# An RWKV-7 scan on one core: the transition and output matrices of each chunk made ahead of the states

## The chip, the cores and the metric

The kernel runs on one core of one Trainium2 chip. The metric is the device time of one execution in microseconds. TensorE (PE in the profile) multiplies, VectorE (DVE) and ScalarE (ACT) copy and do elementwise work, GpSimd (POOL) helps with splits, SyncE (SP) issues the DMAs. "Out<-in" in a row of the profile names the tile that is written and the tiles that are read.

## The reference

One layer of a hybrid encoder trunk on a sequence of 1024 with a width of 1024: an mLSTM branch, a Hyena branch and an RWKV-7 branch read the same normalised input, and their outputs are gated, projected and merged. The change is in the RWKV-7 branch, which scans in both directions over 16 heads of 64:

```python
def rwkv7_scan(r, w, k, v, kk, a, reverse):
    def step(state, inp):
        r_t, w_t, k_t, v_t, kk_t, a_t = inp
        sa = jnp.einsum('bhij,bhj->bhi', state, -kk_t)
        state = (state * w_t[:, :, None, :] + sa[..., None] * (kk_t * a_t)[:, :, None, :]
                 + v_t[..., None] * k_t[:, :, None, :])
        return state, jnp.einsum('bhij,bhj->bhi', state, r_t)
    ...
    y_fwd = rwkv7_scan(r_h, dec_h[:, :, 0], k_dir[:, :, 0], v_h, kk, a_h[:, :, 0], reverse=False)
    y_bwd = rwkv7_scan(r_h, dec_h[:, :, 1], k_dir[:, :, 1], v_h, kk, a_h[:, :, 1], reverse=True)
    y = head_norm(y_fwd + y_bwd, LNX_EPS) * heads(lnx_g) + heads(lnx_b)
```

## The kernel before

**Stages.** The trunk normalises and modulates the input, runs the mLSTM, then the Hyena branch, then the RWKV branch (`rwkv`, from about 830 to 1988 us of the profile), then the merge and the output projection. The input projection, 82 column tiles, is cut into jobs (`gemm`, the tile `pg`, lines 351 to 353: three products of 128x512 for each 128x128 piece of the weights, whose high and low parts ACT and POOL split in lines 333 and 334). Jobs fill TensorE beside the branches: `fill(n)` traces the next `n` pieces of the queue.

**The scan.** Heads are taken in eight pairs, two heads on the 128 partitions (h = 0 and 1). Both directions d of a pair run together. The 1024 positions are 16 chunks of 64; half a direction of a pair (g = 0 and 1) is eight chunks. For each pair `load` fetches k and r, `prep` (four calls: g and d) makes the decayed operands, `tphase` (once for each g) inverts the triangular 64x64 systems of 16 chunks and directions into `tt_t[g]`, `bonus` and `post` do what lies around the scan. `prep` writes `ar` (two halves: kk times decay, and r times decay) and `bk` (two halves: the delta rule's right side b over decay, and k over decay).

`setup(cx, b)` prepares a block b of two chunks, in two parts: the Gram products `pgr` of `bk` and `ar`, masked by DVE into `G`, with the first quarter of `G` overwritten by a copy of `ar` on ACT; then the transposes of `bk` through `ptv` into `B`, and, in the first four blocks, the values (`vp` times `cmat`) into `SV`, whose other half holds the state.

`scan` does 16 steps m, each for one chunk of either direction:

- `U` = products of `G` and `SV`; DVE copies it to `us` (line 1769);
- `SA` = products of `tt_t` and `us`; DVE and ACT copy it into the state's half of `SV` (lines 1775 and 1776);
- `SN` = products of `B` and `SV`; DVE adds the old state `S0` and multiplies by the chunk's decay `pc` (tile `sn`, through `tt`, line 476); DVE and ACT copy it into the next chunk's `SV` (lines 1800 and 1801);
- `own` and `states`, products of `SV` with `G` and of `S0` with `ar`, make the outputs `py`; they are issued one step late, behind `U` and `SA` of the next step. ACT copies them to `y`, or DVE adds them where the other direction was there first.

**Order.** `scan` is a generator with four yields a step. `weave` runs it and, at each yield, runs the generators that `rwkv` has put at that number (`put`: the rest of `prep` of this pair at 0 to 4, `tphase` of the second half at 6 to 26, `load`, `prep` and `tphase` of the next pair later) and an even share of the remaining jobs (`fill`). Between the yields of a step `next(ahead)` runs one part of the next block's `setup`. A scheduler then puts the instructions of each engine into one order at compile time; `in_turn` holds a group of products together (its first product stands in the trace under line 395, the others under 398), and `high_priority` and `issue_after` steer it. On the chip each engine takes its instructions in that order.

**PSUM.** `banks(name)` gives two banks of 512 from one buffer, the tag `a`, which `pq` and `pwx` of `tphase` and `pgr` and `ptv` of `setup` share one after the other. The steps' tile `pch` has two buffers of a bank, the jobs' `pg` three.

Of the kernel before, what the change touches and what calls it, by code (L numbers as in the profile page):

```python
# [18 lines left out]
T = 1024  # L19
# [266 lines left out]
class Trunk:  # L286
# [1060 lines left out]
    def rwkv(self, yc_out, pairs=range(8)):  # L1347
        nc, tc, A = self.nc, self.tc, self.A
        with ExitStack() as c2:
# [17 lines left out]
            self.gmask = cp.tile([128, 2, 128], F32, name="gmask")  # L1367
            nc.sync.dma_start(self.gmask, A["gmask"])
# [21 lines left out]
            cx = [dict(p=p, ar={}, al={}, bk={}, pc={}) for p in pairs]  # L1390
# [10 lines left out]
            for i in range(n):  # L1401
# [7 lines left out]
                put(ahead(tc, self.tphase(cx[i], 1), TP), *range(6, 28, 2))  # L1409
                if i + 1 < n:  # L1410
# [4 lines left out]
                    put(ahead(tc, self.tphase(nx, 0), TP), *range(39, 62, 2))  # L1415
# [118 lines left out]
    def prep(self, cx, g, d):  # L1534
# [46 lines left out]
        for q in range(2):  # L1581
            ar = self.ep.tile([128, 4, 2, CL], F32, name="ar", tag="ar", bufs=8)
            bk = self.ep.tile([128, 4, 2, CL], F32, name="bk", tag="bk", bufs=8)
            cs = slice(4 * q, 4 * q + 4)
            self.stt(ar[:, :, 0, :], c8(rd(kk))[:, cs], -2.0, P[:, cs, 0:64], MUL, MUL)
            self.tt(ar[:, :, 1, :], c8(rd(r))[:, cs], P[:, cs, 1:65])
            self.tt(bk[:, :, 0, :], c8(tmp)[:, cs], s[:, cs, 1:65])

            self.tt(bk[:, :, 1, :] if d == 0 else bk[:, :, 1, ::-1], c8(a)[:, cs], s[:, cs, 1:65])
            for j in range(2):  # L1590
                cx["al"][g, d, 2 * q + j] = ar[:, 2 * j:2 * j + 2, 0, :]
            for j in range(4):
                cx["ar"][g, d, 4 * q + j] = ar[:, j]
                cx["bk"][g, d, 4 * q + j] = bk[:, j]
            yield

    def tphase(self, cx, g):
# [68 lines left out]
    def setup(self, cx, b):  # L1666

        nc, rp, vp = self.nc, self.rp, self.vp
        if b == 0:
# [4 lines left out]
        ops = [(j, d, cx["bk"][g, d, c + j], cx["ar"][g, d, c + j]) for j in range(2) for d in range(2)]  # L1674

        G = rp.tile([128, 2, 2, 2, 128], F32, name="G", tag="G", bufs=2)

        pg = [x.rearrange("p (j d c) -> p j d c", j=2, d=2) for x in self.banks("pgr")]
        self.in_turn(partial(nc.tensor.matmul, pg[h][:, j, d, :], bk[hsl[h]], ar[hsl[h]], start=True, stop=True)
                     for j, d, bk, ar in ops for h in (1, 0))  # L1680
        for h in range(2):
            self.tt(G[:, :, :, h, :], pg[h], self.gmask.unsqueeze(1).broadcast_to([128, 2, 2, 128]))
            for d in range(2):
                nc.scalar.copy(G[0:64, :, d, h, 0:64], cx["al"][g, d, b % 4][hsl[h]])  # L1684
        yield

        B = rp.tile([128, 2, 2, 128], F32, name="B", tag="B", bufs=2)
        pt, pv = self.banks("ptv")  # L1690
        pt = pt.rearrange("p (j d c) -> p j d c", j=2, d=2)
        for j, d, bk, ar in ops:
            nc.tensor.transpose(pt[:, j, d, :], bk.rearrange("p a b -> p (a b)"), self.ident)
        nc.scalar.copy(B, pt)
        if b < 4:

            SV = rp.tile([128, 2, 4, 64], F32, name="SV", tag="SV", bufs=4)
            if b == 0:
                nc.gpsimd.memset(SV[0:64], 0.0)
# [5 lines left out]
            for k in range(2):  # L1705
                nc.scalar.copy(SV[64:128, :, 2 * k:2 * k + 2].rearrange("p h e x -> p e h x"),
# [6 lines left out]
        cx["set"] = (G, B, SV, at)  # L1713
        yield

    def outputs(self, y, py, m, S0, ar, now):

        nc = self.nc
        hsl = (slice(0, 64), slice(64, 128))
        G, B, SV, at, both = now  # L1720

        def own(ins):
            return self.in_turn((partial(nc.tensor.matmul, py[hsl[h], d], SV[:, h, at[d]], G[:, m % 2, d, h, 64:128],
                                         start=m == 0 or d == 0, stop=m == 0)
                                 for d in range(2) for h in range(2)), ins)

        def states(ins):
            self.in_turn((partial(nc.tensor.matmul, py[hsl[h], d], S0[hsl[h], d], ar[d][hsl[h], 1, :],
                                  start=False, stop=d == 1)
                          for d in range(2 if m else 0) for h in range(2)), ins)  # L1730
# [7 lines left out]
        return own, states  # L1738

    def scan(self, cx, nx):  # L1740

        nc, rp = self.nc, self.rp
        S0 = None
        y = rp.tile([128, T], F32, name="y", tag="y", bufs=1)
        hsl = (slice(0, 64), slice(64, 128))

        def chunk(m):

            G, B, SV, at = cx["set"]
            at = at[m % 2]  # L1750
            step = at[1] - at[0]
            return G, B, SV, at, slice(at[0], at[1] + (1 if step > 0 else -1) if at[1] + step >= 0 else None, step)
        now, late = chunk(0), None
        for m in range(16):
            g, c, j = m // 8, m % 8, m % 2
# [160 lines left out]
```

## Time and profile before

| | us |
|---|---|
| median of 3 runs | 2189.37 |
| lowest and highest | 2178.8, 2193.34 |
| the profiled execution | 2200.05 |
| its span from the first to the last instruction | 2198.3 |
| the scan, first step to last, in the profile | 929.5 to 1988 |

The profile records one execution. A row of a view by groups has line, engine, operation, tiles, shape and count, then busy time in us and the mean of one in ns, then the idle time of the engine ahead of it and what ended it. A row of the timeline begins with start and length in us. "128*64 128x64" of a product is its tile of the array, rows times columns, and the shape of what streams through it. One fp32 product of the program is two instructions. A waits row has the waiting engine and line, what it waited for, then us in total, times, and the longest.

### The profile page before, as it was taken

The numbers are of one execution on the slowest core, as the hardware profiler recorded it, in microseconds if no ns is written. First come the engines' busy times: TensorE is split into PE (matmuls) and PEld (weight loads), VectorE is DVE, ScalarE is ACT, GpSimd is POOL, SyncE is SP. The second block draws the span as 40 slices with busy tenths as digits, with TensorE's granted clock in tenths as the row PEclk, the third lists the DMA queues.
The fourth block names the chain that finished last, engine by engine and source line by source line (L and its number), as shares of the span: only waits on it lengthen the run. The fifth ranks groups of instructions, "written<-read, shape, count | busy, mean of one in ns | idle before, by whom it ended". The sixth has DMA issues, their size and how long they took to land. (4 is left out here: it accounts for less than half of the span.)

```text
span 2198.3 us, 45984 instructions
## 1 busy us (share of the span) xinstructions
PE 1994.0 (91%) x17098; PEld 1509.2 (69%) x17098; DVE 1634.6 (74%) x4754; ACT 1103.2 (50%) x2558; POOL 424.3 (19%) x485
## 2 busy tenths in 40 slices
PE   6999899999989899899989999999898887897998
PEld 4666777787868677666766676666666665675786
DVE  4854999988447947788787888868887888764536
ACT  5557356454242115664665756667466564532221
POOL 2211311122222432311101111111114411010200
PEclk9999999999999999999998999999899998897999
DMA  8211222334465345321322333224143542445623
GB/s 255 70 67 59 78 77 90 112 101 127 143 200 172 119 138 163 124 68 61 130 79 93 117 106 102 92 81 136 52 155 118 187 144 63 159 143 175 196 89 129
DMA packets 169384, 262.19 MB, mean 119 GB/s; under 512 B 17863, under 2 KB 87335, under 8 KB 169160
## 3 DMA queue, kind: packets, MB, share of 16 engines
q1 hardware_dynamic: 169160, 259.25, 36.3%
q8 instruction: 135, 2.21, 0.4%
q14 instruction: 89, 0.73, 0.1%
HBM read 181.06 MB, written 78.12 MB: 118 GB/s over the span
## 5 line engine op out<-in xcount | busy, mean ns | idle before, releaser
L334 POOL TENSOR_TENSOR wl<-wraw,wh 128x256 fp32r<-128x256 f32 x408 | 371.5, 915 | 1488.6 <-ACT wh L333 1464.8
L351 PE MATMUL pg<-hh,wh 128*128 128x512 f32 x1440 | 601.5, 418 | 20.9 <-ACT wh L333 11.8
L352 PE MATMUL pg<-hh,wl 128*128 128x512 f32 x1440 | 594.3, 413 | 16.4 <-POOL wl L334 16.3
L353 PE MATMUL pg<-hl,wh 128*128 128x512 f32 x1440 | 592.4, 412 | 1.9 <-DVE hl L565 1.8
L351 PEld LDWEIGHTS pg<-hh,wh 128*128 128x128 f32 x1440 | 278.7, 194 | 88.9 <-ACT wh L333 15.1
L352 PEld LDWEIGHTS pg<-hh,wl 128*128 128x128 f32 x1440 | 279.3, 194 | 78.0 <-POOL wl L334 22.2
L353 PEld LDWEIGHTS pg<-hl,wh 128*128 128x128 f32 x1440 | 278.1, 193 | 62.0 <-DVE hl L565 2.8
L333 ACT CAST wh<-wraw 128x256 fp32r<-128x256 f32 x408 | 162.7, 404 | 220.6 <-PE pg L353 122.1
L476 DVE TENSOR_TENSOR tm<-Ab,Tb 128x126 f32<-128x126 f32 (+22 forms) x496 | 145.4, 293 | 4.4 <-DMA Tb<-in_tinit 2.7
L476 DVE TENSOR_TENSOR Tb<-Tb,tm 128x126 f32<-128x126 f32 (+22 forms) x496 | 144.2, 291 | 1.9
L473 DVE SCALAR_TENSOR_TENSOR st<-pg,hmu,st 128x511 f32<-128x511 f32 (+1 forms) x130 | 80.9, 636 | 27.9 <-ACT e L424 17.6
L476 DVE TENSOR_TENSOR G<-pgr,gmask 128x512 f32<-128x512 f32 x128 | 85.4, 679 | 17.0 <-PE pgr L398 17.0
L457 ACT ACTIVATE st<-pg 128x512 f32<-128x512 f32 x74 | 44.2, 597 | 99.9 <-PE pg L353 95.0
L1684 ACT COPY G<-ar 64x128 f32<-64x128 f32 x256 | 64.3, 295 | 48.4 <-DVE G L476 46.6
L473 DVE SCALAR_TENSOR_TENSOR st<-st,pg 128x512 f32<-128x512 f32 x80 | 54.3, 679 | 35.7 <-PE pg L353 12.7
L398 PE MATMUL pgr<-ar,bk 64*128 64x128 f32 x896 | 76.9, 287 | 0.0
L141 DVE SCALAR_TENSOR_TENSOR row<-row 64x1 f32<-64x1 f32 x393 | 72.7, 208 | 2.1
L1769 DVE COPY us<-pch 128x128 f32<-128x128 f32 x128 | 36.3, 283 | 45.8 <-PE pch L398 45.5
L395 PEld LDWEIGHTS pch<-SV,G 128*64 128x64 f32 x256 | 25.3, 139 | 65.5 <-ACT SV L1801 52.3
L395 PE MATMUL pch<-SV,G 128*64 128x64 f32 x256 | 43.2, 252 | 27.7 <-ACT SV L1801 26.2
L476 DVE TENSOR_TENSOR dw<-dw,dw 128x512 f32<-128x512 f32 x92 | 67.1, 760 | 0.9
L395 PEld LDWEIGHTS pch<-SV,B 128*64 128x64 f32 x256 | 25.3, 139 | 60.1 <-ACT SV L1776 50.1
(677 smaller groups left out, 4228.4 us busy)
## 6 DMA issues: line engine op xcount, KB each, us to landing
wraw<-in_w_in SPq DMA_DIRECT2D x340, 128.0 KB, 2.3
low<-lora SPq DMA_DIRECT2D x32, 512.0 KB, 4.1
sig<-st SPq DMA_DIRECT2D x48, 256.0 KB, 2.6
st<-sig SPq DMA_DIRECT2D x48, 256.0 KB, 3.5
wraw<-in_w_br SPq DMA_DIRECT2D x68, 128.0 KB, 2.8
adw<-in_ada_w SPq DMA_DIRECT2D x16, 512.0 KB, 7.1
x<-in_x SPq DMA_DIRECT2D x8, 512.0 KB, 6.1
hx<-st SPq DMA_DIRECT2D x16, 256.0 KB, 2.0
```

The costliest lines, as they stand in the source:

```text
L141: self.ops.append(lambda: self.nc.vector.scalar_tensor_tensor(o, a, s, b, op0=op0, op1=op1))
L333: self.nc.scalar.copy(hi, raw)
L334: self.nc.gpsimd.tensor_tensor(lo, raw, hi.bitcast(F32), op=SUB)
L351: nc.tensor.matmul(p, wh, hh, start=(k == 0), stop=False)
L352: nc.tensor.matmul(p, wl, hh, start=False, stop=False)
L353: nc.tensor.matmul(p, wh, hl, start=False, stop=(k == n - 1))
L395: ins = f()
L398: ins = f()
L457: self.nc.scalar.activation(o, p, AF.Tanh, scale=0.5)
L473: return self.nc.vector.scalar_tensor_tensor(out, in0, s, in1, op0=op0, op1=op1)
L476: return self.nc.vector.tensor_tensor(out, a, b, op=op)
L1684: nc.scalar.copy(G[0:64, :, d, h, 0:64], cx["al"][g, d, b % 4][hsl[h]])
```

## The change

The state's half and the value's half of `SV` change places. For each chunk and direction the setup now makes the transition matrix `R` (128x64: from state and values to the next state before decay) and the output matrix `Q` (128x64: from state and values to the outputs), and a step has only the products `SN` = R and `SV`, and `py` = `SV` and Q. `SN` is scaled by `pc` while it is copied into the next chunk's `SV`: two scaled copies on ACT for the first head, one on DVE for the second. `U`, `SA`, `us`, the state tile `sn`, and the late outputs are gone.

`setup` has three parts instead of two, each in its own place between yields (the third in the block's second step). First: the products of `ar` with `ki` (tile `px`) and of `be` with `ar` and with the unit matrix (`pb`); DVE masks half of each into `X` and `Gb`, ACT copies the other half. Second: `tt` times `X` into `TX`, and the values. Third: products of `ki` with `ar` and with the unit matrix, and of `TX` with `Gb` added to them, in `pqr`; ACT copies `R`, DVE masks `Q`. So `tt` is read in the setup, not in the step, and `tphase` is put at earlier numbers. `bk` becomes `be` (b over decay) and `ki`, eight standing tiles whose second half POOL fills once with the unit matrix. `tphase` takes the diagonal exchange of its partitions (`o` for `64 * h`) with the same number of products.

```diff
             nc.vector.tensor_scalar(self.hwa, self.col("w0", 0, 32), 0.5, None, op0=MUL)
             self.hlgb = cp.tile([128, 16], F32, name="hlgb")
             nc.vector.tensor_scalar(self.hlgb, self.col("lg", 0, 16), 0.5, None, op0=MUL)
-            self.gmask = cp.tile([128, 2, 128], F32, name="gmask")
-            nc.sync.dma_start(self.gmask, A["gmask"])
+            gm = cp.tile([128, 8, CL], F32, name="gmask")
+            nc.sync.dma_start(gm, A["gmask"])
+            self.mask_x, self.mask_g, self.mask_q, self.eye = gm[:, 0:2], gm[:, 2], gm[:, 3:7], gm[:, 7]
+            self.ki = [self.ep.tile([128, 4, 2, CL], F32, name="ki", tag="bk", bufs=8) for _ in range(8)]
+            for x in self.ki:
+                nc.gpsimd.tensor_copy(x[:, :, 1, :], self.eye.unsqueeze(1).broadcast_to([128, 4, CL]))
...
-                put(ahead(tc, self.tphase(cx[i], 1), TP), *range(6, 28, 2))
+                put(ahead(tc, self.tphase(cx[i], 1), TP), 6, 8, 10, 12, 13, 14, 15, 16, 18, 20, 22)
...
-                    put(ahead(tc, self.tphase(nx, 0), TP), *range(39, 62, 2))
+                    put(ahead(tc, self.tphase(nx, 0), TP), 39, 40, 41, 42, 43, 44, 46, 48, 50, 52, 54)
...
             ar = self.ep.tile([128, 4, 2, CL], F32, name="ar", tag="ar", bufs=8)
-            bk = self.ep.tile([128, 4, 2, CL], F32, name="bk", tag="bk", bufs=8)
+            be = self.ep.tile([128, 4, CL], F32, name="be", tag="be", bufs=8)
+            ki = self.ki[4 * g + 2 * d + q]
             cs = slice(4 * q, 4 * q + 4)
             self.stt(ar[:, :, 0, :], c8(rd(kk))[:, cs], -2.0, P[:, cs, 0:64], MUL, MUL)
             self.tt(ar[:, :, 1, :], c8(rd(r))[:, cs], P[:, cs, 1:65])
...
+            self.tt(be, c8(tmp)[:, cs], s[:, cs, 1:65])
+            self.tt(ki[:, :, 0, :] if d == 0 else ki[:, :, 0, ::-1], c8(a)[:, cs], s[:, cs, 1:65])
             for j in range(4):
                 cx["ar"][g, d, 4 * q + j] = ar[:, j]
-                cx["bk"][g, d, 4 * q + j] = bk[:, j]
+                cx["be"][g, d, 4 * q + j] = be[:, j]
+                cx["ki"][g, d, 4 * q + j] = ki[:, j]
...
@@ -1665,69 +1672,122 @@
     def setup(self, cx, b):
         nc, rp, vp = self.nc, self.rp, self.vp
         if b == 0:
             nc.sync.dma_start(vp, self.krv["v", cx["p"]])
             cx["sv"] = []
         g, c = b // 4, 2 * (b % 4)
         hsl = (slice(0, 64), slice(64, 128))
...
+        ops = [(2 * j + d, 8 * d + c + j) + tuple(cx[n][g, d, c + j] for n in ("ar", "be", "ki"))
+               for j in range(2) for d in range(2)]
+        mm = lambda o, l, r, start=True, stop=True: partial(nc.tensor.matmul, o, l, r, start=start, stop=stop)
+        px, pb = (x.rearrange("p (i c) -> p i c", c=128) for x in self.banks("pxb"))
+        def grams():
+            for i, u, ar, be, ki in ops:
+                for h in range(2):
+                    yield mm(px[hsl[1 - h], i], ar[hsl[h], 0, :], ki[hsl[h]].rearrange("p a b -> p (a b)"))
+                for h in range(2):
+                    yield mm(pb[hsl[h], i, 0:64], be[hsl[h]], ar[hsl[h], 1, :])
+                for h in range(2):
+                    yield mm(pb[hsl[h], i, 64:128], be[hsl[h]], self.eye[hsl[h]])
+        self.in_turn(grams())
+        X = rp.tile([128, 4, 128], F32, name="X", tag="X", bufs=1)
+        Gb = rp.tile([128, 4, 128], F32, name="Gb", tag="Gb", bufs=1)
+        dm = lambda x: x.rearrange("p (j d) t -> p j d t", d=2)
+        self.tt(dm(X[:, :, 0:64]), dm(px[:, :, 0:64]), self.mask_x.unsqueeze(1).broadcast_to([128, 2, 2, CL]))
+        nc.scalar.copy(X[:, :, 64:128], px[:, :, 64:128])
+        self.tt(Gb[:, :, 0:64], pb[:, :, 0:64], self.mask_g.unsqueeze(1).broadcast_to([128, 4, CL]))
+        nc.scalar.copy(Gb[:, :, 64:128], pb[:, :, 64:128])
         yield
-        B = rp.tile([128, 2, 2, 128], F32, name="B", tag="B", bufs=2)
+        tt = self.tt_t[g]
         pt, pv = self.banks("ptv")
-        pt = pt.rearrange("p (j d c) -> p j d c", j=2, d=2)
-        for j, d, bk, ar in ops:
-            nc.tensor.transpose(pt[:, j, d, :], bk.rearrange("p a b -> p (a b)"), self.ident)
-        nc.scalar.copy(B, pt)
+        pt = pt.rearrange("p (i c) -> p i c", c=128)
+        self.in_turn(mm(pt[hsl[h], i], tt[hsl[1 - h], u, :], X[hsl[1 - h], i]) for i, u, *_ in ops for h in range(2))
+        TX = rp.tile([128, 4, 128], F32, name="TX", tag="X", bufs=1)
+        nc.scalar.copy(TX, pt)
         if b < 4:
             SV = rp.tile([128, 2, 4, 64], F32, name="SV", tag="SV", bufs=4)
             if b == 0:
-                nc.gpsimd.memset(SV[0:64], 0.0)
+                nc.gpsimd.memset(SV[64:128], 0.0)
             cx["sv"].append(SV)
             pv = pv[:, 0:256].rearrange("p (e c) -> p e c", e=2)
             for e in range(2):
                 t0 = 128 * (7 - b if e else b)
                 nc.tensor.matmul(pv[:, e], vp[:, t0:t0 + 128], self.cmat, start=True, stop=True)
             for k in range(2):
-                nc.scalar.copy(SV[64:128, :, 2 * k:2 * k + 2].rearrange("p h e x -> p e h x"),
+                nc.scalar.copy(SV[0:64, :, 2 * k:2 * k + 2].rearrange("p h e x -> p e h x"),
                                pv[hsl[k]].rearrange("p e (h x) -> p e h x", h=2))
             at = ((0, 3), (2, 1))
             SV = cx["sv"][b]
         else:
             SV = cx["sv"][7 - b]
             at = ((1, 2), (3, 0))
-        cx["set"] = (G, B, SV, at)
         yield
-    def outputs(self, y, py, m, S0, ar, now):
-        nc = self.nc
+        pq = [x.rearrange("p (i c) -> p i c", c=128) for x in self.banks("pqr")]
+        def both():
+            for i, u, ar, be, ki in ops:
+                for n, r in enumerate((ar[:, 1, :], self.eye)):
+                    for h in range(2):
+                        yield mm(pq[h][:, i, 64 * n:64 * n + 64], ki[hsl[h]].rearrange("p a b -> p (a b)"), r[hsl[h]],
+                                 i + n == 0, False)
+            for i, *_ in ops:
+                for h in range(2):
+                    yield mm(pq[h][:, i], TX[hsl[h], i], Gb[hsl[h], i], False, i == 3)
+        self.in_turn(both())
+        R = rp.tile([128, 2, 4, CL], F32, name="R", tag="R", bufs=2)
+        Q = rp.tile([128, 2, 4, CL], F32, name="Q", tag="Q", bufs=1)
+        for h in range(2):
+            nc.scalar.copy(R[:, h], pq[h][:, :, 64:128])
+            self.tt(Q[:, h], pq[h][:, :, 0:64], self.mask_q)
+        cx["set"] = (Q, R, SV, at)
+        yield
+    def scan(self, cx, nx):
+        nc, rp = self.nc, self.rp
+        y = rp.tile([128, T], F32, name="y", tag="y", bufs=1)
         hsl = (slice(0, 64), slice(64, 128))
...
+        def chunk(m):
+            Q, R, SV, at = cx["set"]
+            at = at[m % 2]
+            step = at[1] - at[0]
+            return Q, R, SV, at, slice(at[0], at[1] + (1 if step > 0 else -1) if at[1] + step >= 0 else None, step)
+        now = chunk(0)
+        for m in range(16):
+            g, c, j = m // 8, m % 8, m % 2
+            Q, R, SV, at, _ = now
+            if j == 0:
+                ahead = self.setup(cx, m // 2 + 1) if m < 14 else self.setup(nx, 0) if nx else iter(())
+            ch = self.ps.tile([128, 2, 2, CL], F32, name="pch", tag="c", bufs=2)
+            SN, py = ch[:, 0], ch[:, 1]
+            ins = None
+            if m < 15:
+                ins = self.in_turn(partial(nc.tensor.matmul, SN[hsl[h], d], R[:, h, 2 * j + d], SV[:, h, at[d]],
+                                           start=True, stop=True) for d in range(2) for h in range(2))
+            self.in_turn((partial(nc.tensor.matmul, py[hsl[h], d], SV[:, h, at[d]], Q[:, h, 2 * j + d],
+                                  start=True, stop=True) for d in range(2) for h in range(2)), ins)
+            yield
+            next(ahead, None)
+            yield
+            if m < 15:
+                now = chunk(m + 1)
+                SV, at, to = now[2:]
+                pc = cx["pc"][g][:, :, c:c + 1]
+                for d in range(2):
+                    nc.scalar.activation(SV[64:128, 0, at[d]], SN[0:64, d], AF.Copy, scale=pc[0:64, d])
+                self.tt(SV[64:128, 1, to], SN[64:128], pc[64:128].broadcast_to([64, 2, CL]))
             for d, n in enumerate((m, 15 - m)):
                 ysl = y[:, 64 * n:64 * n + 64]
                 src = py[:, d] if d == 0 else py[:, d, ::-1]
...
```

The steps that follow in `scan` (the outputs into `y` and the last two yields) stand as before. `gmask` on the host becomes the four masks and the unit matrix.

More of the change, by code (lines that the diff above doesn't have):

```diff
@@ L1389, in rwkv @@
             n = len(pairs)
-            cx = [dict(p=p, ar={}, al={}, bk={}, pc={}) for p in pairs]
+            cx = [dict(p=p, ar={}, be={}, ki={}, pc={}) for p in pairs]
             run(self.load(cx[0]))
@@ L1673, in setup @@
         hsl = (slice(0, 64), slice(64, 128))
[L1674 to L1684, printed above, removed]
+        ops = [(2 * j + d, 8 * d + c + j) + tuple(cx[n][g, d, c + j] for n in ("ar", "be", "ki"))
+               for j in range(2) for d in range(2)]
@@ L1737, in states @@
                     self.tt(ysl, ysl, src, ADD)
[L1738 to L1755, printed above, removed]
-            tt = self.tt_t[g]
-            ar = [cx["ar"][g, d, c] for d in range(2)]
-            G, B, SV, at, both = now
-            if j == 0:
-                ahead = self.setup(cx, m // 2 + 1) if m < 14 else self.setup(nx, 0) if nx else iter(())
-            ch = self.ps.tile([128, 4, 2, CL], F32, name="pch", tag="c", bufs=2)
-            U, SA, SN, py = (ch[:, i] for i in range(4))
-            ins = self.in_turn(partial(nc.tensor.matmul, U[hsl[h], d], G[:, j, d, h, 0:64], SV[:, h, at[d]],
-                                       start=True, stop=True) for d in range(2) for h in (1, 0))
-            if late:
-                late[0](ins)
-            us = self.sm.tile([128, 2, CL], F32, name="us", tag="us", bufs=2)
-            nc.vector.tensor_copy(us, U)
-            ins = self.in_turn(partial(nc.tensor.matmul, SA[hsl[h], d], tt[hsl[h], 8 * d + c, :], us[hsl[h], d],
-                                       start=True, stop=True) for d in range(2) for h in range(2))
-            if late:
-                late[1](ins)
-            late = None
-            nc.vector.tensor_copy(SV[0:64, 0, both], SA[0:64])
-            nc.scalar.copy(SV[0:64, 1, both], SA[64:128])
-            yield
-            next(ahead, None)
-            yield
-            self.in_turn(partial(nc.tensor.matmul, SN[hsl[h], d], B[:, j, d, hsl[h]], SV[:, h, at[d]],
-                                 start=True, stop=True) for d in range(2) for h in (1, 0))
-            S1 = self.sm.tile([128, 2, 64], F32, name="sn", tag="sn", bufs=3)
-            pc = cx["pc"][g][:, :, c:c + 1].broadcast_to([128, 2, 64])
-            if m == 0:
-                self.tt(S1, SN, pc)
-            else:
-                self.tt(S1, SN, S0, ADD)
-                self.tt(S1, S1, pc)
-            late = self.outputs(y, py, m, S0, ar, now)
-            S0 = S1
-            if m < 15:
-                now = chunk(m + 1)
-            if m in (7, 15):
-                late[1](late[0](None))
-                late = None
-            if m < 15:
-                SV, at = now[2], now[4]
-                nc.vector.tensor_copy(SV[0:64, 0, at], S1[0:64])
-                nc.scalar.copy(SV[0:64, 1, at], S1[64:128])
```

32 lines of the change are left out of this document (12 added, 20 removed).

## The prediction

> **What bounds the kernel now.** The page comes first:
>
> ```profile
> PE 1994.0 (91%) x17098; PEld 1509.2 (69%) x17098; DVE 1634.6 (74%) x4754; ACT 1103.2 (50%) x2558; POOL 424.3 (19%) x485
> ```
>
> TensorE looks full, but its products are pipelined and the record counts their tails, so this 91% bounds nothing. What the change touches runs from 929.5 to 1988 us, eight pairs of heads of 16 steps each; the groups by tile show that nothing on `pch`, `G` or `B` lies before or after it, save one setup. The busy times by window, cut where a pair's first `us` copy starts, with a stretch before the phase as the last row (columns: length, then busy time and count of PE, weight loads, DVE, ACT, POOL, granted clock, DMA):
>
> ```profile
> 929.50:1055.70 126.20, 117.88 (x1547) 86.88 (x1547) 99.73 (x312) 68.47 (x183) 17.54 (x24) 0.95 0.23 77
> 1055.70:1193.30 137.60, 125.55 (x1566) 93.35 (x1566) 108.49 (x324) 82.57 (x204) 17.08 (x23) 0.93 0.29 93
> 1193.30:1323.30 130.00, 122.15 (x1586) 89.51 (x1588) 105.56 (x319) 85.08 (x205) 16.43 (x23) 1.00 0.33 107
> 1323.30:1459.50 136.20, 127.50 (x1603) 93.29 (x1599) 109.75 (x329) 83.13 (x207) 22.11 (x28) 1.00 0.31 101
> 1459.50:1594.10 134.60, 120.50 (x1552) 89.18 (x1554) 111.16 (x325) 84.31 (x203) 14.98 (x22) 0.94 0.27 87
> 1594.10:1750.40 156.30, 135.25 (x1607) 98.64 (x1609) 131.47 (x326) 99.78 (x238) 56.41 (x61) 0.96 0.46 149
> 1750.40:1884.70 134.30, 115.11 (x1523) 85.23 (x1525) 111.45 (x332) 75.82 (x187) 15.09 (x21) 0.90 0.37 119
> 1884.70:1988.00 103.30, 93.71 (x1192) 68.39 (x1192) 67.56 (x203) 44.55 (x128) 10.02 (x13) 0.93 0.42 135
> ...
> 660.00:740.00 80.00, 75.32 (x319) 60.61 (x319) 65.65 (x89) 19.47 (x42) 24.33 (x25) 0.98 0.55 173
> ```
>
> DVE is busy for 0.79, 0.79, 0.81, 0.81, 0.83, 0.84 and 0.83 of the first seven pairs and 0.65 of the last. For TensorE I count what its instructions occupy, from start to start, in the timeline of one step:
>
> ```profile
> 1210.43 0.27 PE L395 MATMUL pch<-SV,G 128*64 128x64 f32 x1 [0.80 <-ACT SV L1801]
> ...
> 1211.05 0.51 PE L353 MATMUL pg<-hl,wh 128*128 128x512 f32 x1
> ...
> 1211.71 0.27 PE L395 MATMUL pch<-us,tt 64*64 64x64 f32 x1
> 1211.72 0.27 PE L398 MATMUL pch<-us,tt 64*64 64x64 f32 x1
> ...
> 1212.33 0.50 PE L352 MATMUL pg<-hh,wl 128*128 128x512 f32 x1
> ...
> 1214.78 0.27 PE L395 MATMUL pch<-SV,B 128*64 128x64 f32 x1 [1.04 <-ACT SV L1776]
> ...
> 1215.16 0.50 PE L1552 MATMUL plw<-low,w2h 128*128 128x512 f32 x1
> 1215.50 0.60 PE L1693 MATMUL ptv<-ident,bk 128*128 128x128 f32 x4
> 1215.85 0.48 PE L1552 MATMUL plw<-low,w2l 128*128 128x512 f32 x1
> ...
> 1216.40 0.39 PE L352 MATMUL pg<-hh,wl 128*128 128x512 f32 x1
> 1216.63 0.39 PE L353 MATMUL pg<-hl,wh 128*128 128x512 f32 x1
> ...
> 1218.35 0.71 PE L1704 MATMUL ptv<-cmat,vp 128*128 128x128 f32 x4
> 1218.81 0.48 PE L351 MATMUL pg<-hh,wh 128*128 128x512 f32 x1
> ...
> 1220.98 0.37 PE L395 MATMUL pgr<-ar,bk 64*128 64x128 f32 x1
> ...
> 1222.07 0.27 PE L395 MATMUL pch<-SV,B 128*64 128x64 f32 x1
> ```
>
> A wide product (128x512) occupies 0.23 us (1216.40 to 1216.63). The products `U` with the outputs `own` take 0.62 (1210.43 to 1211.05), `SA` with `states` 0.62 (1211.71 to 1212.33), `SN` 0.38 (1214.78 to 1215.16): 1.62 a step. A block of two steps adds its Gram products (`pgr`) 1.09, four transposes 0.35, and in half of the blocks the value products 0.46. `tphase` adds:
>
> ```profile
> 1467.47 0.24 PE L395 MATMUL pq<-ar,bk 64*32 64x64 f32 x1
> ...
> 1469.38 0.27 PE L395 MATMUL pch<-us,tt 64*64 64x64 f32 x1
> ```
>
> Its 128 products take 1.91 us; its two groups of 64 I put at 1.2 each by that row. A pair thus has 16 x 40 scan instructions, 8 x 20 of setup, 16 of values and 512 of `tphase`, about 1,320 in all, which occupy 16 x 1.62 + 8 x 1.44 + 4 x 0.46 + 2 x 4.3 = 48 us. The rest of the PE count in a window row are wide products: 227, 246, 266, 283, 232, 287 and 203. The pairs hold 100, 105, 109, 113, 101, 114 and 95 us of work for TensorE, together 737 of 955 us: 0.79, 0.76, 0.84, 0.83, 0.75, 0.73 and 0.70 of their length.
>
> So **two engines are near their limit together**. Pairs 5 to 7 have little for TensorE and are no shorter: there DVE, at 0.83 to 0.84, sets the time. In pairs 3 and 4 both stand above 0.8. What is left is waiting for one another:
>
> ```profile
> DVE us L1769 <- PE pch L398: 45.5, 45, 3.5
> PEld pch L395 <- ACT SV L1801: 52.3, 71, 5.8
> PEld pch L395 <- ACT SV L1776: 50.1, 82, 2.2
> ```
>
> The reader sees a round trip: PE waits for a copy, whose engine waits for PE, three times a step.
>
> **The change part by part.** *Steps.* `U`, `SA`, `SN`, `own` and `states` (40 instructions) become `SN` and the outputs (16 of the `SV,G` kind, 0.62). TensorE saves 1.0 us a step, 2.0 a block. Two of three round trips go.
>
> *Setup.* Gone are `pgr` and the transposes, 1.44. In come three groups.
>
> The first has 24 products in 64x64 tiles, 48 instructions. All four tiles are used, each for about 0.22 us per chunk and direction: two of the 0.11 that a pair takes in `pgr` (1.09 for eight pairs, less some 0.2 of start), or four half as wide. `pq` shows that tiles of one row group run beside each other: 128 products in 1.91 us is 15 ns each, which two at a time would not reach. So 4 x 0.23 + 0.2 of start = 1.15; two tiles at a time would give 2.0.
>
> The second (`TX`) has 16 instructions 128 wide, like `pgr`: 1.09.
>
> The third has 32 instructions 64 wide and 16 that are 128 wide, all with 128 columns of weights. What do 128 columns cost when little streams through them?
>
> ```profile
> L737 PEld LDWEIGHTS pdc<-de,ident x16: 183/187/189, 273.4 to 275.1; 64*128 64x128 f32 x16
> ```
>
> Sixteen products of only 8 columns start from 273.4 to 275.1 us, 0.113 apart, as slow as 128 columns do: the weight load sets the pace. So 24 pairs of two row groups at 0.111 + 0.2 = 2.85; if the load were hidden, 2.0. I take 2.85, for this row has the same 64x128 weights.
>
> A block's setup goes from 1.44 to 5.09 and its steps from 3.24 to 1.24: **+1.65 us of TensorE a block** (0.8 to 2.5), 13 us a pair.
>
> Here a page speaks against the change. The Trainium skill, TensorEngine Tiling (Array Packing), Restrictions and Gotchas, says that different row tiles cannot access one PSUM bank at the same time. By it the first two groups would run one row group at a time. The rows speak against that: `us,tt` has both row groups writing one bank, and its first two products start 10 ns apart (1211.71, 1211.72).
>
> *DVE.* Out go:
>
> ```profile
> L476 DVE TENSOR_TENSOR G<-pgr,gmask 128x512 f32<-128x512 f32 x126 | 84.1, 678 | 15.9 <-PE pgr L398 15.9
> L476 DVE TENSOR_TENSOR sn<-sn,pc 128x128 f32<-128x128 f32 x120 | 37.3, 311 | 0.6
> L1769 DVE COPY us<-pch 128x128 f32<-128x128 f32 x128 | 36.3, 283 | 45.8 <-PE pch L398 45.5
> L1775 DVE COPY SV<-pch 64x128 f32<-64x128 f32 x128 | 35.3, 276 | 25.5 <-PE pch L398 24.5
> L476 DVE TENSOR_TENSOR sn<-pch,sn 128x128 f32<-128x128 f32 x120 | 34.0, 283 | 39.1 <-PE pch L398 32.7 <-ACT st L457 5.0 <-ACT wh L333 0.8
> L1800 DVE COPY SV<-sn 64x128 f32<-64x128 f32 x120 | 27.3, 228 | 1.2 <-PE pch L398 0.7
> ```
>
> That is 254 us. In come four masked copies of 128x256 a block; between 0.283 for 128 elements and 0.678 for 512 this is 0.41 each, 106 us in all, and one scaled 64x128 copy a step, 0.28 x 120 = 34. Net -114, 14 a pair; the records of neighbours overlap a little, so -90 is the lower end. DVE falls from 845 to about 731 us.
>
> *ACT.* Out go:
>
> ```profile
> L1684 ACT COPY G<-ar 64x128 f32<-64x128 f32 x252 | 63.3, 295 | 48.1 <-DVE G L476 46.3
> L1694 ACT COPY B<-ptv 128x512 f32<-128x512 f32 x63 | 36.8, 584 | 19.5 <-PE ptv L1693 18.9
> ```
>
> 100 us, and two `SV` copies a step for two scaled ones of half the width, about even. In come four 128x256 copies (0.37 each by interpolation) and one 128x512 (0.58) a block, 132. ACT rises by some 30 from 624 of 1058, which DVE and PE cover; without that cover it is late by those 30.
>
> *Queues.* `tphase` must end some steps earlier, since setup now reads `tt`; it is the same work, in a denser stretch of a DVE with 14 us less to do: nothing, or 2 us a pair if that stretch is full. The new `SN` on PE waits for the scaled copies, with wide products queued behind it; a whole step of other work lies between, where `SA` had only what was pulled ahead. POOL makes eight unit blocks first: 8 x 1.1 us beside the weight splits, which wide products wait for there:
>
> ```profile
> 748.17 3.49 POOL L334 TENSOR_TENSOR wl<-wraw,wh 128x256 fp32r<-128x256 f32 x3 [0.59 <-ACT wh L333]
> ```
>
> I take 3 (0 to 9). The first setup, with nothing beside it, is longer by about 3. No DMA is added or moved.
>
> *Sum.* The seven full pairs hold 737 + 7 x 13 = 828 us for TensorE. At today's length that is 0.87, while DVE is at 0.69: TensorE becomes the bound. How full can it get? In the 80 us ahead of the phase 319 wide products ran: 73 us, 0.92, with DVE at 0.82. The phase has shorter groups and more hand-overs, but its best pairs reach 0.84 with DVE as the other limit. I take 0.88: 828 / 0.88 = 941, -14. By pair: the first, third and fourth get 2 to 8 us longer, pairs 5 to 7 5 to 12 shorter. The last pair loses one or two round trips a step at its end, where nothing else runs: -5. With +6 at the start: -13. The profiled execution took 2200.05 us (span 2198.3); it lies 10.7 above the median of 2189.37, so the median after is 2176. A measurement can tell about 1%, 22 us, from no change.
>
> **The rivals.** *TensorE at 0.85 to 0.91 (the forecast):* 974 to 910 for the seven pairs, -47 to +24 in all, 2142 to 2213. Chance 0.51: 0.19 faster by over 1%, 0.29 within, 0.03 slower.
>
> *The waits melt.* Three round trips a step were the trouble; with one, TensorE is filled to 0.94 and its clock stays up: it is 1.00 in pairs 3 and 4 and 0.90 to 0.96 elsewhere, where TensorE stood still more often. 828 / 0.94 = 881, -74 and -5 at the end: 2110. For: DVE sets pairs 5 to 7. Against: 0.94 is above anything in this trace. The Trainium skill, TensorE: Matmul & The Clock Gate, Part 1, says that activity releases the throttle; the clock column agrees. Chance 0.22.
>
> *The setup chain decides (slower).* All three stages go through the one pair of banks `a`, each waits for the copies of the one before, and TensorE stands still in its queue meanwhile. Work alone: 1.15 + 0.85 + 1.09 + 0.6 + 2.85 + 0.85 = 7.4 us, `tphase` about 2 a block, of 16.5 us. It decides from hand-overs (five a block) of over 1.4 us. The wait rows have 45.5 us in 45 waits, 1.0, and longer ones where DVE is behind. At 1.6 the block grows by 1.0, +64: 2253; TensorE at 0.82 gives 1010, +55, much the same: 2244. For: one buffer, more stages. Against: the stages are a quarter of a block apart. Chance 0.24.
>
> *Row tiles share no bank.* 0.9 us more in each of two groups, 64 x 1.8 = 115, and by 0.88 +131: 2307. Against it stands the 10 ns. Chance 0.03.
>
> *The range* goes from 2110 to 2250: below lies a third of the second case, above half of the third and the last. The setup's bounds, 0.8 and 2.5 a block, shift the sum by -62 and +62 at 0.88, within it.
>
> **What would show it.** Right: `pqr` groups 2.7 to 3.0 us long, the first group 1.1 to 1.3, DVE at 720 to 750 us over the phase, pairs 5 to 7 shorter and 3 and 4 not. Wrong: `pqr` near 2.0 (the load hides); DVE still over 0.8; large waits of PE for `X` or `TX` (the chain); a clock of 1.00 all through with TensorE above 0.91 (the waits melt).

## The result, and the profile after

The changed kernel takes 2470.7 us (median of four runs, 2465.0 to 2475.7) against 2191.3 beside it: 1.129 times as long, with an interval of 1.124 to 1.134. The prediction, 2176 in a range of 2110 to 2250, was wrong in sign and size. The profiled execution has a span of 2468.4 us, against 2198.3.

The page's line of engines, and the busy times by window, cut again at the pairs (length, then PE, weight loads, DVE, ACT, POOL with counts, granted clock, DMA):

```profile
PE 2160.5 (88%) x19914; PEld 1682.4 (68%) x19914; DVE 1601.8 (65%) x4378; ACT 1117.1 (45%) x2548; POOL 415.4 (17%) x493
```

```profile
923.00:1082.00 159.00, 141.24 (x1910) 108.89 (x1911) 94.51 (x262) 72.16 (x184) 17.03 (x24) 0.94 0.20 63
1082.00:1253.00 171.00, 154.99 (x2022) 118.86 (x2018) 111.55 (x286) 88.43 (x211) 20.62 (x29) 0.96 0.26 88
...
1596.00:1782.00 186.00, 153.59 (x1937) 117.83 (x1941) 114.80 (x275) 99.90 (x234) 47.12 (x54) 0.93 0.33 108
...
1956.00:2134.00 178.00, 128.91 (x1766) 104.47 (x1761) 104.95 (x276) 75.29 (x178) 9.23 (x13) 0.70 0.22 73
2134.00:2258.00 124.00, 91.58 (x1298) 78.78 (x1294) 44.23 (x131) 40.06 (x111) 1.01 (x1) 0.62 0.15 51
sum 1335.00, PE 1121.95 PEld 876.25 DVE 805.95 ACT 635.89 POOL 160.18; mean PE 140.24 PEld 109.53 DVE 100.74 ACT 79.49 POOL 20.02
```

All of the loss lies in the scan's phase: 1335 us against 1058.5, every full pair 18 to 51 us longer. DVE's share falls from about 0.8 to 0.6. Priced as the prediction prices it (0.23 us for each of the 1886 and 1875 wide products, and the start-to-start time of each small group), TensorE's work in the phase rises from about 811 to 903 us: 0.77 of the phase before and 0.68 after. So some 92 us are work. The other 185 or so are waiting, and products that ran slower: the granted clock is 0.88 over the phase, against 0.95 before. The waits of the phase:

```profile
DVE ki L476 <- PE pqr L398: 124.0, 13, 14.0
DVE Q L476 <- ACT R L1749: 104.4, 48, 17.1
...
PE pwx L395 <- DVE t L1648: 57.4, 15, 10.8
PE ptv L395 <- ACT Gb L1704: 40.8, 26, 3.9
...
ACT tt L1662 <- DVE t L1651: 75.7, 13, 11.4
```

In the kernel before, the wait of `pwx` for `t` is small:

```profile
PE pwx L395 <- DVE t L1641: 2.3, 6, 0.6
```

Thirteen waits of up to 14 us (the first row) are something else than hand-overs. They fall at the same two places of the pairs, the setups of blocks 3 and 7. One of them in the timeline (start, length, engine, line, operation, tiles; in brackets the idle time and what ended it; rows of PE, DVE and ACT):

```profile
1374.69 0.32 PE L395 MATMUL pxb<-ki,ar 64*64 64x128 f32 x1
...
1386.80 1.05 DVE L1648 STREAM_TRANSPOSE t<-Tb 128x512 f32<-128x512 f32 x1
1388.00 0.23 PE L395 MATMUL pwx<-t,q 32*32 32x32 f32 x1 [3.29 <-DVE t L1648]
1389.95 0.58 ACT L1661 COPY W<-pwx 32x512 f32<-32x512 f32 x1 [4.23 <-PE pwx L398]
1394.35 0.21 PE L395 MATMUL pwx<-t,W 32*32 32x32 f32 x1
1395.59 1.17 ACT L1670 COPY tt<-pwx 32x512 f32<-32x512 f32 x2 [1.96 <-PE pwx L398]
1397.06 0.32 PE L395 MATMUL ptv<-X,tt 64*64 64x128 f32 x1
1399.20 0.32 PE L395 MATMUL pqr<-ar,ki 64*128 64x64 f32 x1
1400.81 0.43 DVE L476 TENSOR_TENSOR ki<-a,s 128x256 f32<-128x256 f32 x1 [10.40 <-PE pqr L398]
1402.53 0.36 ACT L1749 COPY R<-pqr 128x256 f32<-128x256 f32 x1
1402.97 0.33 PE L395 MATMUL pch<-SV,R 128*64 128x64 f32 x2
```

Block 7's first group `pxb` is done by 1376; its second, `ptv`, starts at 1397. In between stands `pwx`, the end of the *next* pair's `tphase`, which waits until DVE has finished its chain and transposes. Meanwhile TensorE uses up jobs, until it stands still at 1384.7. Block 7 reads the other `tt_t` and needs nothing of it. But `pxb`, `pwx`, `ptv` and `pqr` all take the one buffer `a`. Block 7 issues its parts behind numbers 48, 50 and 52, and the new numbers put `pwx` at 50 and 52; for block 3 they are 16, 18, 20 and 18, 20. In the kernel before it stood at 22 and 24, behind block 3, and at 55 and 57, behind block 7, so late that `t` was mostly ready. The next step cannot start before R, at 1402.5, and DVE, in its order, stands 10.4 us behind a write of `ki` that waits for this same `pqr`.

### The profile page after: what moved, and what is told of

Read it like the earlier page. It is cut to its first block, busy times and chain, and to the rows that moved or that the text cites. A ratio compares the mean times of both kernels' runs of the same rounds, so it can differ in the third digit from the quotient of the medians.

```text
span 2468.4 us, 51153 instructions
## 1 busy us (share of the span) xinstructions
PE 2160.5 (88%) x19914; PEld 1682.4 (68%) x19914; DVE 1601.8 (65%) x4378; ACT 1117.1 (45%) x2548; POOL 415.4 (17%) x493
## 5 line engine op out<-in xcount | busy, mean ns | idle before, releaser
L476 DVE TENSOR_TENSOR Q<-pqr,gmask 128x256 f32<-128x256 f32 x128 | 53.7, 419 | 108.6 <-ACT R L1749 108.4
L398 PE MATMUL pqr<-ar,ki 64*128 64x64 f32 x896 | 115.7, 306 | 0.0
L398 PE MATMUL pqr<-gmask,ki 64*128 64x64 f32 x1024 | 113.1, 302 | 0.0
L1749 ACT COPY R<-pqr 128x256 f32<-128x256 f32 x128 | 47.2, 369 | 137.0 <-PE pqr L398 111.5
L476 DVE TENSOR_TENSOR ki<-a,s 128x256 f32<-128x256 f32 x64 | 28.3, 450 | 124.2 <-PE pqr L398 124.0
L1789 ACT ACTIVATE SV<-pch,pc 64x64 f32<-64x64 f32 x240 | 62.4, 302 | 74.8 <-PE pch L398 72.2
L398 PEld LDWEIGHTS pqr<-gmask,ki 64*128 64x128 f32 x1024 | 91.4, 217 | 0.0
L398 PEld LDWEIGHTS pqr<-ar,ki 64*128 64x128 f32 x896 | 90.0, 216 | 0.0
L398 PE MATMUL pch<-SV,R 128*64 128x64 f32 x720 | 59.2, 253 | 28.8 <-ACT R L1749 23.8
L398 PE MATMUL pqr<-Gb,TX 64*128 64x128 f32 x1024 | 84.0, 312 | 0.0
```

Source lines behind the costliest of these rows:

```text
L398: ins = f()
L476: return self.nc.vector.tensor_tensor(out, a, b, op=op)
L1749: nc.scalar.copy(R[:, h], pq[h][:, :, 64:128])
L1789: nc.scalar.activation(SV[64:128, 0, at[d]], SN[0:64, d], AF.Copy, scale=pc[0:64, d])
```

## The experiments

Theories at the start: **order** (the place of `pwx` in the turn of `a`), **tt** (setup reads `tt` sooner and it isn't ready), **ki** (DVE held by the standing tiles). Ratios are to the kernel before, run beside each.

**e1_between**: `tphase`'s last parts between two blocks.

```diff
-TP), 6, 8, 10, 12, 13, 14, 15, 16, 18, 20, 22)
+TP), 6, 8, 10, 12, 13, 14, 15, 16, 22, 23, 24)
-TP), 39, 40, 41, 42, 43, 44, 46, 48, 50, 52, 54)
+TP), 39, 40, 41, 42, 43, 44, 46, 48, 54, 55, 56)
```

> The changed kernel with the last three parts of tphase put at 22, 23, 24 and 54, 55, 56 instead of 18, 20, 22 and 50, 52, 54, so that pwx stands between two blocks' setups and no longer between the first and the second part of blocks 3 and 7. Theory order (the pair of PSUM banks that all of them share makes the second part of those setups wait for tphase's chain, and the steps behind it too): the two stalls of some 30 us a pair go, the steps' phase falls from 1335 us to 1100-1180 and the time to 2240-2320 us. Theory tt (setup reads tt two steps sooner than the steps did, and tphase isn't ready): the wait only moves to block 4 and block 0 of the next pair, time 2420-2500. Theory ki (DVE stands in its order behind the standing tiles ki, which wait for pqr): the 124 us of that wait stay, time 2400-2480.

2345.0 us, 1.071 (1.065 to 1.076): 126 us back. That is 25 us above the range of **order**, and far below the two others. The waits of `ki` are down to one:

```profile
DVE ki L476 <- PE pqr L398: 0.4, 1, 0.4
```

So `ki` was a victim of the stall and not its cause, and **ki** falls.

**e2_tt_constant**: the data dependence taken out, the order kept.

```diff
-tt[hsl[1 - h], u, :], X[hsl[1 - h], i])
+self.cmat[hsl[1 - h], 0:64], X[hsl[1 - h], i])
```

> The changed kernel with tt in the setup's second part replaced by a constant matrix, so that no setup waits for the data of tphase; the output isn't the reference's. All else, the order of the PSUM pair among it, is as in the changed kernel. Theory order: nothing changes, 2440-2500 us, and the wait of pwx for DVE's t stays near 57 us. Theory tt: the stalls go, 2200-2320 us. Theory ki: 2400-2480.

2484.6 us, 1.135 (1.130 to 1.140), no gain, with the same waits:

```profile
PE pwx L395 <- DVE t L1648: 54.2, 14, 9.7
...
DVE ki L476 <- PE pqr L398: 124.9, 13, 14.0
```

The theory **tt** falls: the setup that no longer reads `tt` waits as long.

**e3_before_numbers** and **e14_before_between**: the move alone, in the kernel before. One of the two lines is shown; the other moves `tphase(nx, 0)` to its numbers in the same way:

```diff
-self.tphase(cx[i], 1), TP), *range(6, 28, 2))
+self.tphase(cx[i], 1), TP), 6, 8, 10, 12, 13, 14, 15, 16, 18, 20, 22)     # e3; e14: ..., 16, 22, 23, 24
```

> The kernel before with tphase put at the changed kernel's numbers and nothing else changed: pwx comes to stand between the two parts of blocks 3 and 7 (pgr and ptv). Theory order: it slows, to 2270-2400 us, since B of these blocks is then late. Theory tt: tt is first read in step 8, the tphase is only earlier, 2170-2215. Theory ki: no such tiles here, 2170-2215.

> The kernel before with tphase at the denser numbers, but its last parts at 22, 23, 24 and 54, 55, 56, between two blocks, as in e1. Theory order: the 80 us that e3 lost are gone, 2180-2205 us. Theory density: 2225-2270.

e3: 2268.3 us, 1.038 (1.033 to 1.044), 2 us below the range of **order**. e14: 2184.9, 0.9987 (0.9963 to 1.0011). The denser stretch costs nothing; the places of its last parts cost 80 us. The waits of e3, then of e14, for the end of DVE's chain and for what block 3 or 7 holds up:

```profile
PE pwx L395 <- DVE t L1641: 14.5, 10, 3.4
...
DVE bk L476 <- PE ptv L1693: 24.3, 5, 7.4
```

```profile
PE pwx L395 <- DVE t L1641: 1.9, 5, 0.6
```

**e4_own_bank** and **e8_bank_and_between**: `pwx` leaves `a`. The changed `pch` is half a bank, so its two buffers fit into one.

```diff
+self.pch = self.ps.tile([128, 2, 2, 2, CL], F32, name="pch", tag="c", bufs=2)
+self.pwx = self.ps.tile([128, NT], F32, name="pwx", tag="c", bufs=2)
-pw, px = (... for x in self.banks("pwx"))
+pw = px = self.pwx.rearrange("p (u t) -> p u t", t=32)
-ch = self.ps.tile([128, 2, 2, CL], F32, name="pch", tag="c", bufs=2)
+ch = self.pch[:, m % 2]
```

> The changed kernel, its numbers kept, with a PSUM bank of pwx's own (both of tphase's last products use it one after the other; the steps' pch takes the two halves of one bank in turn instead of two banks). Theory order: ptv and pxb no longer wait for pwx, 2230-2320 us, and no wait of ptv of blocks 3 and 7 behind pwx. Theory tt: b 4 and b 0 wait for tt as before, 2420-2490. Theory ki: 2400-2480.

> e4_own_bank with tphase's last parts put between the blocks as in e1: both cures of the order together. If the bank pair was all that tphase disturbed, no more than e4 gives: 2275-2305 us by either theory. If tphase's place costs something besides (DVE's and ACT's order), it differs by over 25 us from e4.

e4: 2289.7 us, 1.047 (1.042 to 1.052), 181 us back with the numbers unchanged. e8: 2298.2, 1.052 (1.048 to 1.055), no more. The phase is 1141 us, the wait for `t` is a quarter of what it was, and the low clock of the last two pairs is gone (0.91 and 0.97 from 1800 to 1960 and to 2063 us of e4):

```profile
918.30:2059.20 1140.90, 1018.23 (x14781) 787.15 (x14781) 788.71 (x2070) 629.34 (x1527) 157.69 (x206) 0.96 0.30 97
```

```profile
PE pwx L395 <- DVE t L1650: 13.9, 11, 2.2
```

**Order** is shown. In e4's trace `pwx` stands behind the last products of block 3 or 7 throughout the phase, at unchanged numbers: with a bank of its own it is free to be put there at compile time. e1, which keeps the one buffer, is some 45 us slower than e8, so the shared turn costs something between blocks too. The Trainium skill, Perfetto Trace Analysis, Optimization Strategy, says that a gap repeating for a stretch can mean that there is not enough PSUM for the next tile; the trace agrees, with two gaps in nearly every pair and 181 us gone with one bank more. Some 100 us over the kernel before are left.

The next runs weigh **work** (TensorE's added products), **chain** (the length of the setup's chain) and **hand-over** (copies that run one behind another).

**e5_outputs_twice** and **e9_one_product**: TensorE's work up and down, both from e4 (operands shortened):

```diff
 # e5
-... for d in range(2) for h in range(2)), ins)
+... for _ in range(2) for d in range(2) for h in range(2)), ins)
 # e9: a standing tile holds k, unit, r; b takes r's place in ar
-for n, r in enumerate((ar[:, 1, :], self.eye)):
-    ... mm(pq[h][:, i, 64 * n:64 * n + 64], ki, r[hsl[h]], ...)
+    ... mm(pq[h][:, i], ki[:, 0:2], ki[:, 1:3], ...)
-    mm(pb[.., 0:64], be, ar[.., 1, :]); mm(pb[.., 64:128], be, self.eye)
+    mm(pb[.., i], be, ki[:, 1:3])
```

> e4_own_bank with the four output products py of each step made twice (same result, 8 products of some 0.04 us more a step behind SN, 42 to 48 us of TensorE in the phase, off the setup's chain). Theory work (what is left of the loss, some 100 us, is TensorE's added work at the share of 0.76 that it also had before): 2335-2355 us against 2290 of e4. Theory chain (the block's chain through the one PSUM pair, pxb, copies, ptv, copy, pqr, copies, sets the pace and TensorE has room): 2285-2305.

> e4_own_bank with r moved into the standing tiles behind the unit matrix (k, unit, r), so that unit and r are one operand of 128 columns: 8 products of pxb and 16 of pqr less a block, TensorE's work down by 0.75 to 1.0 us a block, 48 to 64 us in the phase; b takes r's old place. Theory work: 2205-2240 us. Theory chain: the pqr of the chain is shorter by the same 0.75, so 2220-2260.

e5: 2321.6 us, 1.061 (1.056 to 1.067), between the two ranges. The step's 16 instructions in 0.615 us became 24 in 0.848, +30 us in the phase; the time rose by 32. e9: 2269.9, 1.038 (1.034 to 1.043), above both ranges. `pqr` fell from 2.88 to 1.985 and `pxb` from 1.09 to 1.03, 61 us in the phase; the time fell by 20. A microsecond of TensorE cost about one in e5 and a third of one in e9: neither theory alone holds.

**e6_chain_short**: `ptv` in the bank of `pwx`, the `ki` products of `pqr` ahead of `TX`'s copy, from e8.

```diff
-pt, pv = self.banks("ptv")
+pt, pv = self.pwx, None          # values: a tile of tag b
 ...                              # second part, behind the values:
+self.in_turn(keys())             # the ki products of pqr
 yield
```

> e4_own_bank with tphase's last parts put between the blocks as in e1, ptv in the bank of pwx so that it no longer waits for the copies out of pxb, the values in the bank of phs and plw, and the ki products of pqr issued in the second part right behind ptv, under TX's copy. The same work on each engine, and a chain some 2.8 us a block shorter (1.8 of pqr, about 1 of the copies of Gb). Theory work: 2265-2300 us. Theory chain: up to 180 us less than e8, 2120-2230.

2305.9 us, 1.055 (1.051 to 1.059), against 1.052 of e8: nothing gained, and far from the range of **chain**. At the same work, the length of the setup's chain does not set the pace.

**e10_r_q_whole**: one copy and one mask for both heads, from e9.

```diff
-for h in range(2):
-    nc.scalar.copy(R[:, h], pq[h][:, :, 0:64])
-    self.tt(Q[:, h], pq[h][:, :, 64:128], self.mask_q)
+nc.scalar.copy(R, pq[:, :, :, 0:64])
+self.tt(Q, pq[:, :, :, 64:128], self.mask_q...)
```

> e9_one_product with both heads' R copied in one ACT copy and both heads' Q masked in one DVE operation (instead of R, Q, R, Q, which stand one behind another in the trace). Theory hand-over (what is left of the loss is in copies out of one PSUM pair that run one behind another across ACT and DVE): R is whole some 0.8 us sooner in each block, 15-50 us less than e9's 2270. Theory work (TensorE's products only): 2260-2280.

2243.1 us, 1.026 (1.021 to 1.032), 27 less than e9. One block of e9, then one of e10:

```profile
1443.00 1.06 PE L398 MATMUL pqr<-Gb,TX 64*128 64x128 f32 x16
1444.10 0.37 ACT L1748 COPY R<-pqr 128x256 f32<-128x256 f32 x1 [2.47 <-PE pqr L398]
...
1446.85 0.42 DVE L476 TENSOR_TENSOR Q<-pqr,gmask 128x256 f32<-128x256 f32 x1
1447.30 0.37 ACT L1748 COPY R<-pqr 128x256 f32<-128x256 f32 x1 [2.37 <-DVE Q L476]
...
1447.72 0.39 PE L398 MATMUL pch<-SV,R 128*64 128x64 f32 x5 [1.39 <-ACT R L1748]
```

```profile
1433.02 1.06 PE L398 MATMUL pqr<-Gb,TX 64*128 64x128 f32 x16
1434.12 0.59 ACT L1749 COPY R<-pqr 128x512 f32<-128x512 f32 x1 [1.70 <-PE pqr L398]
1436.61 0.68 DVE L476 TENSOR_TENSOR Q<-pqr,gmask 128x512 f32<-128x512 f32 x1
```

In e9 the second head's R, in another bank, waits 2.4 us for the first head's Q on a DVE that is busy with other work, and TensorE waits for that R: R is whole 3.6 us behind the last product. In e10 it is whole 0.6 us behind it. Over the 64 blocks of each trace the mean goes from 3.6 to 1.6 us. The Trainium skill, PSUM — Partial Sum Buffer, PSUM bank collisions raise a hardware error, says that the compiler's scheduler makes two instructions of different engines wait for one another where they touch the same bank and quadrant. That covers Q behind its own head's R; the 2.37 us wait between two banks is in the rows and not in that rule.

**e11_x_gb_whole** (from e10, `X` and `Gb` by one DVE operation each), **e12_states_on_dve** (from e11, the states' copies by two on DVE), **e13_old_numbers** (e10 with `range(6, 28, 2)` and `range(39, 62, 2)`):

```diff
 # e11
-self.tt(dm(X[:, :, 0:64]), ...); nc.scalar.copy(X[:, :, 64:128], ...)
+self.tt(dm(X), dm(px), self.mask_x...)          # Gb likewise
 # e12
-for d in range(2): nc.scalar.activation(SV[64:128, 0, at[d]], SN[0:64, d], AF.Copy, scale=pc[0:64, d])
+self.tt(SV[64:128, 0, to], SN[0:64], pc[0:64]...)
```

> e10 with X and Gb made by one DVE operation each (masks widened by ones) instead of a DVE mask and an ACT copy each. Theory hand-over: two hand-overs of ACT and DVE fewer between pxb and ptv, some 1 us a block, 10-50 us less than e10. Theory work: within 10 us of e10.

> e11 with the scaled copies of both heads' states into SV on DVE (one operation a head, instead of two on ACT and one on DVE, which stand one behind another). Theory hand-over: some 0.5 us a step, up to 60 us less than e11. Theory work: within 10 us of e11.

> e10_r_q_whole with tphase put at the numbers of the kernel before (6 to 26 and 39 to 61 in steps of two). Theory density (tphase's denser stretch costs by itself, by holding DVE and ACT): 2200-2225 us. Theory order (only the place of pwx in the PSUM pair's order counted, and e10 has that cured by a bank): 2230-2255. If tt comes too late for block 4 by these numbers: over 2265.

2248.6, 2246.9 and 2246.3 us (1.027, 1.026, 1.027): three times no change. Fewer hand-overs of this kind bring no more, against the theory **hand-over**, and `tphase`'s density again costs nothing.

**e15_after_no_loop** and **e16_before_no_loop**: 30 of the 31 rounds of DVE's chain in `tphase` left out of e10 and of the kernel before.

```diff
 for l in range(31):
+    if l:
+        if l % 5 == 4:
+            yield
+        continue
```

> e10_r_q_whole with 30 of the 31 rounds of tphase's inversion on DVE left out (the output isn't the reference's): 60 of 62 DVE operations of a tphase, some 17 us of DVE time twice a pair, and the latency of that chain. Theory DVE (what sets a pair's length is still DVE's order with this chain in it, as in the kernel before): 150-250 us less than e10, 2000-2090. Theory setup (the setup's and steps' hand-overs on PE and ACT set it): less than 80 us less, 2165-2230.

> The kernel before with the same 30 rounds left out (the output isn't the reference's). Theory DVE: 150-250 us less, 1940-2040, and less or more than e15 as the rest of the two kernels' work goes. Theory setup: it falls by more than e15 does, since its setup is shorter.

2192.2 us, 0.9995 (0.9968 to 1.0023), and 2113.5, 0.965 (0.961 to 0.969). The kernel before gains 76 us, e10 51, where the theory **DVE** gave 150 to 250. Part of DVE's chain is on the path of both, yet it does not set the difference between the kernels, which grows from 54 to 79 us without it.

**e18_chain_again** (e6's cures on e12), **e19_setup_earlier** (e10, each part of the setup one place earlier, Q masked in a part of its own, and `tphase`'s last parts as in e1), **e20_both**; of e19's edit only the main line is shown:

```diff
 # e19
-if j == 0: ahead = self.setup(cx, m // 2 + 1) ...
+if j: ahead = self.setup(cx, m // 2 + 2) ...     # ahead of the step's last part
```

> e12_states_on_dve with e6's cures on top (tphase's last parts between the blocks, ptv in pwx's bank, the ki products of pqr right behind ptv). In e6 they gave nothing. Theory setup chain (the pair of banks a is now the tight place, since the copies are shorter): 20-60 us less than e12's 2247. Theory late R (a step waits for R because the setup starts too late in the order, not because it is long): within 15 us of e12.

> e10_r_q_whole with every part of the setup one place earlier between the yields (the first part in the second step of the block before, so that R is whole a half step sooner; Q is masked in a part of its own), and tphase's last parts between the blocks. The same operations. Theory late R (the 57 us of waits of SN for R and Q in PE and its weight loads are the rest of the loss): 25-60 us less than e10's 2243, at or under the kernel before. Theory work (no place to gain, PE's added products at its old share): 2230-2250.

> e18 with the setup's parts one place earlier as in e19. Theory late R: as e19, 2180-2220. Theory setup chain: as e18 or lower. If neither holds: 2230-2250.

2266.5, 2239.2 and 2269.0 us (1.037, 1.024 (1.021 to 1.026), 1.036). e18 is slower than either of its theories gave, and e20 is as slow as e18. An earlier setup gains nothing that can be measured, and e6's cures cost some 20 on e12. No version with the new matrices that computes the reference's output comes below the kernel before. **Open** is what holds e10 and e19 50 us above it. In e10 TensorE's work, priced as above, is 824 us, 13 more than before, and fills 0.75 of the phase, against 0.77. The idle time ahead of its products grew from 100 to 145 us. The largest waits stand ahead of the outputs (for Q), `TX`'s products (for `Gb`), `SN` (for R) and `pwx`:

```profile
PE pch L398 <- DVE Q L476: 25.4, 17, 2.9
PE ptv L395 <- ACT Gb L1704: 24.5, 27, 2.1
PE pch L395 <- ACT R L1749: 21.1, 14, 3.3
PE pwx L395 <- DVE t L1650: 17.8, 10, 2.5
```

None of the single causes tried takes all of that away. Not tried: a Q that DVE masks sooner in its order, or a second buffer for Q and `Gb`, which have one each where `G` and `B` had two.

## Why the prediction was wrong

**The step that failed** is the one under *Queues*: "`tphase` must end some steps earlier ... it is the same work, in a denser stretch ...: nothing, or 2 us a pair". Its sentence on density was right (e13, e14). But it priced the move by DVE's time and looked past only the engines' queues. It left out the turn of `a`, although the text ahead of it names that buffer's users. The two places a pair in that turn cost 181 us in this kernel (e4) and 80 in the kernel before (e3).

**The sum** failed too. "I take 0.88" for TensorE's fill went by the best pairs and by a stretch outside the phase, where the seven pairs as a whole had 0.77 (737 of 955 us). Measured by the same prices: 0.68, and 0.74 to 0.78 with the order cured (e19, e10, e4). Fewer round trips a step did not raise it. At 0.77 the prediction's own 828 us of work need some 1073, 118 more than before, which gives about 2305 (an estimate): close to e4, 2290. So a fill that stays as it was would account for most of what e4 leaves; that TensorE's work is the cause is not shown, since e5 and e9 price it differently.

**The slower rival** had the right place, the one pair of banks, and the wrong holder. It counted the setup's own stages and hand-overs. Of these, only a sooner R gained (e10, 27 us); e6 and e18 shorten the chain and gain nothing. What decided was a foreign stage in their midst that waits for DVE. Its 2244 meets e10 by chance.

**The sizes** of the new work held. `pqr` 2.88 us (2.85 predicted), the first group 1.09 (1.15), `TX` 1.02 (1.09), `SN` and outputs 0.615 (0.62). The new copies:

```profile
L476 DVE TENSOR_TENSOR Q<-pqr,gmask 128x256 f32<-128x256 f32 x126 | 52.8, 419 | 104.5 <-ACT R L1749 104.4
L1711 ACT COPY TX<-ptv 128x512 f32<-128x512 f32 x63 | 37.0, 587 | 64.9 <-PE ptv L398 64.8
L476 DVE TENSOR_TENSOR SV<-pch,pc 64x128 f32<-64x128 f32 x118 | 34.8, 295 | 70.8 <-ACT SV L1789 67.9
```

0.42, 0.59 and 0.30 us against 0.41, 0.58 and 0.28. TensorE's work rose by some 92 us where 106 were predicted. DVE's busy time fell by 39 us, from 845 to 806, not by 114: the lengths of its records fell by 120 in sum (1001 to 881), but neighbours overlap in them, by 156 us before and by 75 after. POOL's unit blocks took 0.41 us each and not 1.1, a size that no row gave, and the phase began 9 us earlier (929.0 to 919.6), not 6 later. By its own terms the forecast's band is -44 to +20, not -47 to +24.

**Row tiles share no bank**, the rival of 2307, is out: the first group with its two banks and four tiles took 1.09 us, not 2.0.

**The waits melt** did not come: the scan's waits for `us` and `SA` went, but waits for R and `Gb` came in their place, and TensorE was not filled.

## What to carry to other kernels

Where a step is moved in an order written by hand, list the rotating buffers that it is moved past as well as the engines. A buffer with one place makes an order among users that share no data, and one that waits holds up all behind it. Price such a move by making it alone in the kernel before: e3 and e14 differ in six numbers and 83 us. The fill of an engine at its best stretch is no forecast for the stretch that is to change.

## What was not expected of the hardware

The granted clock fell to 0.70 and 0.62 in the last two pairs, which have the same stalls and the fewest wide products to cover them: 104 products of jobs, against 329 before, since the first six pairs had taken 1581 of them, against 1371. In the kernel before the clock was 0.90 and 0.93 there, and it is 0.96 over e4's whole phase. The Trainium skill, TensorE: Matmul & The Clock Gate, Part 1, says that activity releases the throttle; these rows agree in direction. Part of a stall's price is paid in the work that follows it. In the stall shown above, TensorE stands still for 3.3 us ahead of `pwx`. The windows ahead of this gap, behind it, and behind that (granted clock before the last two numbers):

```profile
1380.00:1384.70 4.70, 4.70 (x21) 3.53 (x19) 4.49 (x11) 1.22 (x3) 2.23 (x3) 1.00 0.16 46
1388.00:1393.40 5.40, 5.40 (x72) 4.59 (x73) 2.33 (x5) 3.38 (x6) 0.00 (x0) 0.50 0.53 168
1393.40:1397.00 3.60, 3.60 (x74) 2.65 (x72) 0.00 (x0) 1.39 (x3) 0.00 (x0) 0.96 0.03 7
```

Wide products start 0.23 us apart in the first and the third, and 0.43 apart in the second. What this adds up to over the phase was not measured.

Halving the instructions of `pqr`'s first part at the same number of streamed columns (32 of 64 columns, then 16 of 128) took 0.9 us off 2.88: an instruction with 128 streamed columns costs about as much as one with 64, 0.06 us (2.88 us for 48, 1.985 for 32). Both have 128 columns of weights, so what streams through does not set the pace here; that the weight load does, as the prediction took it, fits these figures.
